# Hybrid encoder trunk: both heads of a pair walked together in the attention mixers, the state space scan given out in four phases

## The chip, the cores and the metric

One Trainium2 chip, one core. Its engines run side by side: TensorE (PE, with its weight loads as PEld), VectorE (DVE), ScalarE (ACT), GpSimd (POOL) and SyncE (SP), which issues the loads from HBM. Each has its own queue and works through it in order; between engines semaphores set the order. The metric is the device time of one execution in microseconds (us).

## The reference

Two layers over 512 tokens of width 1024, in float32. The mixers of a layer are what the change touches:

```python
for i in range(DEPTH):
    h = rms_norm(x, g_mix[i])
    x = x + hybrid_mixer(h, ...)
    h = rms_norm(x, g_ffn[i])
    x = x + (swiglu(h, ...) if i % 2 == 0 else moe_swiglu(h, ...))
    x = x + (p[i] @ ple_w_up[i]) * sigmoid(rms_norm(x, g_ple[i]) @ ple_w_gate[i])

def hybrid_mixer(h, ...):
    (u, fq, fk, fv, ff, cq, ckv, kpe, dq, dk, dv) = split(h @ w_in)
    y_a = s5_mixer(u, ...)                              # state space scan, then GLU
    y_b = fox_mixer(fq, fk, fv, ff, b_f)                # 4 heads, decay, frame causal
    y_c = mla_mixer(cq, ckv, kpe, ...)                  # 4 heads, low rank, chunk causal
    y_d = chunk_band_attention(dq, dk, dv, rel_bias)    # 4 heads, relative bias
    for bi, y in enumerate((y_a, y_b, y_c, y_d)):
        merged += sigmoid(h @ w_gate[bi] + b_gate[bi]) * (y @ w_branch[bi])
    return merged @ w_o
```

The attention mixers: for each head, softmax(q k^T / sqrt(d) + bias or decay, masked) times v. The scan: x_t = a x_(t-1) + B u_t over complex states, y = C x + D u, then y = gelu(y), y * sigmoid(y @ w_glu).

## The kernel before

All activations lie transposed in SBUF (features on partitions, 512 tokens along the row). Dense projections get float32 accuracy from two parts of each operand: `mm3` (lines 153 to 155) issues three matmuls, hi*hi, hi*lo, lo*hi. A weight tile is loaded by SP (`load`, line 130), its hi part is cast by ACT (line 133), its lo part by DVE (line 135); a ring holds four such tiles. PSUM has two pools of four banks: pool a (`bank_a`), from which the projections take theirs, and pool b (`bank_b`), from which scores, transposes, value products and the scan take theirs. A pool gives its banks out in turn, in the order of the program's text.

A scheduler orders the instructions of each engine when the program is built. It may put later instructions, such as projections that need only a bank of pool a and a weight tile, between the steps of an earlier part that has to wait.

A layer's mixer runs in the text in this order: the values of chk (branch 3); two chk pairs (`unit_chk`), with `s5_prep` after the first (it builds the tables of the scan in `s5_maps`, DVE lines 355 to 392); the gates and products of branch 3; two fox pairs (`unit_fox`), the gates and products of branch 1; two mla pairs (`unit_mla`); the scan (`s5`); gates and products of branch 2; gates and products of branch 0. `gates` runs eight projections, 24 matmuls each; `product` eight of six matmuls.

`attention` handles one head; a pair calls it twice. It goes through four query blocks b of 128 rows, with n = 128(b+1) keys. For each: scores on PE (line 580), a mask on PE for fox (582) and mla (584) or a bias added by DVE for chk (589), the maximum on DVE (591), the exponential with its sum on ACT (592), the reciprocal (593) and the scaling (594) on DVE, one transpose on PE for each 128 keys (597) into a bank of pool b, the evacuation to PT by ACT or DVE in turn by block (600, 602), and the value products on PE (604), which put the head's 64 rows on its half of yps. So there are 96 such blocks in the program: two layers, three kinds of attention, four heads, four blocks.

`s5` stands in one piece: u (466), the maps W on PE (472), the vector work and the scan on DVE (484 to 499), y4 on PE (506 to 508), gelu, the copies to gT (514), the GLU's matmuls on PE (518). The matmul of an attention or the scan has float32 operands; the trace has two records for many of these.

Of the kernel before, what the change touches and what calls it, by code (L numbers as in the profile page):

```python
# [11 lines left out]
F = mybir.dt.float32  # L12
# [3 lines left out]
AF = mybir.ActivationFunctionType  # L16
OP = mybir.AluOpType
AX = mybir.AxisListType
# [4 lines left out]
S = 512  # L23
# [20 lines left out]
def trunk(ctx, tc, I, out, dbg=None):  # L44
    nc = tc.nc
    act = nc.scalar.activation
    tt = nc.vector.tensor_tensor
    ts = nc.vector.tensor_scalar
# [3 lines left out]
    mm = nc.tensor.matmul  # L52
# [13 lines left out]
    small = pool("small", 2)  # L66
# [4 lines left out]
    def bank_a():  # L71
        return pa.tile([128, 512], F, name="a", tag="a")

    def bank_b():
        return pb.tile([128, 512], F, name="b", tag="b")
# [23 lines left out]
    ident = cst[:, 0:128]  # L99
# [140 lines left out]
    ident_b = const.tile([128, 128], BF, name="ident_b")  # L240
    caus_b = const.tile([128, 128], BF, name="caus_b")
    tri_b = const.tile([128, 128], BF, name="tri_b")
    onesm_b = const.tile([128, 128], BF, name="onesm_b")
    half_b = const.tile([1, 128], BF, name="half_b")
    neg_b = const.tile([1, 64], BF, name="neg_b")
# [202 lines left out]
    def s5(l, u_src, yT, tt_pool):  # L448
        with new_pool("s5") as p:
            def tile8(nm, tag=None):  # L450
                return p.tile([128, 8, 128], F, name=nm, tag=tag or nm)
# [12 lines left out]
            for g in range(4):  # L464
                for j in range(4):
                    cp[(4 * g + j) % 3](U4[32 * j:32 * j + 32, g::4, :], u5[32 * g:32 * g + 32, :, :, j])
            wps = []
            for c, PT in enumerate((PT0, PT1)):
                for h in range(2):
                    ps = bank_b()  # L470
                    for a in range(4):
                        mm(ps[:, a * 128:(a + 1) * 128], PT[:, 4 * h + a, :], U4[:, 4 * h + a, :],
                           start=True, stop=True)
# [17 lines left out]
            for z, w in ((zr, W[0]), (zi, W[1])):  # L491
                nc.vector.tensor_tensor_scan(out=fl(w), data0=fl(R), data1=fl(z), initial=0.0,
                                             op0=OP.mult, op1=OP.add)
            Xr, Xi = zr, zi
            for Xc, a, b, o in ((Xr, 0, 1, OP.subtract), (Xi, 1, 0, OP.add)):
                nc.vector.memset(Xc[:, :, 0:1], 0.0)
                tt(out=Xc[:, :, 1:128], in0=Er[:, :, 0:127], in1=W[a][:, :, 0:127], op=OP.mult)
                tt(out=z1[:, :, 0:127], in0=Ei[:, :, 0:127], in1=W[b][:, :, 0:127], op=OP.mult)
                tt(out=Xc[:, :, 1:128], in0=Xc[:, :, 1:128], in1=z1[:, :, 0:127], op=o)
            y4 = tile8("y4", "z1")  # L500
            for h in range(2):
                ps = bank_b()
# [9 lines left out]
            for g in range(4):  # L512
                for i in range(4):
                    cp[(4 * g + i) % 3](g5[32 * g:32 * g + 32, :, :, i], y4[32 * i:32 * i + 32, g::4, :])
            for m in range(2):
                ps = bank_b()
                for k in range(2):
                    mm(ps, wg[:, k, m * 128:(m + 1) * 128], gT[:, k, :], start=(k == 0), stop=(k == 1))
                th_ = p.tile([128, S], F, name="th", tag=f"W{m}")
                act(th_, ps, AF.Tanh, scale=0.5)  # L520
                stt(th_, th_, 1.0, gT[:, m, :], op0=OP.add, op1=OP.mult)
                split(th_, yT[0][:, m, :], yT[1][:, m, :], scale=0.5)
# [48 lines left out]
            tt(out=xs, in0=xs, in1=ps, op=OP.add)  # L571
        return f

    def attention(ap, kind, qk, V, vh, yps, a, T):
        for b in range(4):
            n = 128 * (b + 1)
            s = bank_b()
            qs = slice(b * 128, (b + 1) * 128)
            for i, (qT, kT) in enumerate(qk):
                mm(s[:, :n], qT[:, qs], kT[:, :n], start=(i == 0), stop=(kind == "chk" and i == len(qk) - 1))  # L580
            if kind == "fox":
                mm(s[:, n - 128:n], ident_b, caus_b, start=False, stop=True)
            if kind == "mla":
                mm(s[:, n - 64:n], half_b, neg_b, start=False, stop=True)
            mx = small.tile([128, 2], F, name="mx", tag="mx", bufs=6)
            src = s
            P = ap.tile([128, S], F, name="P", tag="P", bufs=3)
            if kind == "chk":
                tt(out=P[:, :n], in0=s[:, :n], in1=T[:, S - n:S], op=OP.add)
                src = P  # L590
            nc.vector.tensor_reduce(out=mx[:, 0:1], in_=src[:, :n], axis=AX.X, op=OP.max, negate=True)  # L591
            act(P[:, :n], src[:, :n], AF.Exp, bias=mx[:, 0:1], accum_out=mx[:, 1:2])  # L592
            nc.vector.reciprocal(mx[:, 1:2], mx[:, 1:2])
            ts(P[:, :n], P[:, :n], mx[:, 1:2], None, op0=OP.mult)
            pt = bank_b()
            for kb in range(b + 1):
                nc.tensor.transpose(pt[:, kb * 128:(kb + 1) * 128], P[:, kb * 128:(kb + 1) * 128], ident)
            PT = ap.tile([128, S], F, name="PT", tag="PT", bufs=3)
            if b % 2:
                act(PT[:, :n], pt[:, :n], AF.Copy)  # L600
            else:
                nc.vector.tensor_copy(PT[:, :n], pt[:, :n])
            for kb in range(b + 1):
                mm(yps[64 * a:64 * a + 64, qs], V[:, kb, vh * 64:(vh + 1) * 64], PT[:, kb * 128:(kb + 1) * 128],  # L604
                   start=(kb == 0), stop=(kb == b))

    def mixer(l, N, nxt):
        with ExitStack() as mx_stack:
# [19 lines left out]
            def y_tiles():  # L628
                return (yp.tile([128, 2, S], FR, name="y_hi", bufs=2), yp.tile([128, 2, S], FR, name="y_lo", bufs=2))

            def gates(bi, dst, after=None):
                g = []
                for m in range(NK):
                    ps = bank_a()
                    w = load(I["w_gate"][l, bi, m], [128, NK, 128], after=after if m < 3 else None)
                    for k in range(NK):
                        mm3(ps, at(w, ALL, k, ALL), at(hT, ALL, k, ALL), start=(k == 0), stop=(k == NK - 1))
                    t_ = dst(m)
                    act(t_, ps, AF.Tanh, scale=0.5, bias=bg[:, bi, m:m + 1])
                    g.append(t_)  # L640
                return g
# [24 lines left out]
            ap = at_stack.enter_context(new_pool("at"))  # L666
# [83 lines left out]
            def unit_chk(cp, pr, V, yT):  # L750
                q2 = [qk_tile(cp, f"dq{a}", 9) for a in range(2)]

                def cq(ps):
                    for a in range(2):
                        own, oth = halves(a)
                        act(q2[a][own], ps[own], AF.Copy, scale=0.125)
                    for a in range(2):
                        own, oth = halves(a)
                        stt(q2[a][oth], ps[own], 0.125, q2[a][own].bitcast(F), op0=OP.mult, op1=OP.subtract)

                in_tile(l, 6 + pr, hT, cq, hi_after=evacs[3] if pr else None)
                k2 = [qk_tile(cp, f"dk{a}", 9) for a in range(2)]
                kl = qk_tile(cp, "dl", 9)

                def ck(ps):
                    for a in range(2):
                        own, oth = halves(a)
                        act(k2[a][own], ps[own], AF.Copy)
                        act(k2[a][oth], ps[own], AF.Copy)
                    for a in range(2):  # L770
                        own = halves(a)[0]
                        marks.append(tt(out=kl[own], in0=ps[own], in1=k2[a][own].bitcast(F), op=OP.subtract))

                in_tile(l, 8 + pr, hT, ck, hi_after=evacs[3] if pr else None)
                yps = bank_b()
                for a in range(2):
                    h = 2 * pr + a
                    own = halves(a)[0]
                    T = cp.tile([128, S], F, name="T", tag="T", bufs=2)
                    nc.sync.dma_start(out=T, in_=I["chk_T"][l, h])  # L780
                    nc.vector.memset(T[0:64, 448:512], NEG)
                    attention(ap, "chk", [(q2[a], k2[a]), (q2[a][own], kl[own])], V, h, yps, a, T)
                split(yps, yT[0][:, pr, :], yT[1][:, pr, :])

            def unit_fox(fp, pr, V, yT):
# [22 lines left out]
                in_tile(l, 4 + pr, hT, con(1.0, cumk, 1))  # L808
                yps = bank_b()
                (q1, q2), (k1, k2) = tiles  # L810
                for a in range(2):
                    attention(ap, "fox", [(q1[a][0:96], k1[a][0:96]), (q2[a], k2[a])], V, 2 * pr + a, yps, a, None)
                split(yps, yT[0][:, pr, :], yT[1][:, pr, :])

            def unit_mla(mp, pr, V, yT, wuq, wuk):
# [22 lines left out]
                    nc.vector.tensor_copy(ks[a][0:64], ps[64 * a:64 * a + 64])  # L838
                    nc.gpsimd.tensor_copy(ks[a][64:96], krot[32 * a:32 * a + 32])
                yps = bank_b()  # L840
                for a in range(2):
                    attention(ap, "mla", [(qs[a][0:96], ks[a][0:96])], V, 2 * pr + a, yps, a, None)
                split(yps, yT[0][:, pr, :], yT[1][:, pr, :])

            V = values(1)
# [43 lines left out]
                in_tile(l, m, hT, lambda ps: act(dst, ps, AF.Copy))  # L889

            yA = y_tiles()
            s5(l, u_src, yA, tp)
            g = gates(2, ring)
            product(2, yC, g, False)
            g = gates(0, ring)
            product(0, yA, g, False)
            tp_stack.close()
            mT = hT
# [989 lines left out]
```

## Time and profile before

| | us |
|---|---|
| median of three runs | 2049.72 |
| lowest, highest of the three | 2049.27, 4567.53 |
| profiled execution, its own time | 2048.55 |
| span of the profiled execution | 2046.8 |

The mean granted clock of PE in the profiled execution is 0.995 of full speed. In layer 0 the chk stage lies at 56 to 189 us of the span, fox at 189 to 262, mla at 262 to 358, the scan and its neighbours behind it up to about 425; layer 1 repeats them some 929 us later. The stretch 650 to 700 lies in layer 0's feed-forward part and holds projections alone. Times in the rows are us from the start of the span; "busy" counts an instruction from its start to its modelled end, so that the busy times of consecutive matmuls overlap, and a price for one is read from start to start.

### The profile page before, as it was taken

Reading aid. Unit: us, or ns where it says so; the run is one execution under the profiler, and the core shown is the slowest. Engines: PE = TensorE matmul, PEld = TensorE weight load, DVE = VectorE, ACT = ScalarE, POOL = GpSimd, SP = SyncE. Lnnn points to the kernel's source line nnn. Section 1 sums busy time; section 2 is a strip of 40 time slices with the busy share of each in tenths; the row PEclk is TensorE's granted clock in tenths of the full one; section 3 lists DMA queues with packets and bytes.
Section 4 is the critical chain, followed back from the end, with each engine's and each line's share of the span. In section 5 each row is a group of like instructions: output and inputs, shape, how many; then the busy total and the mean of one; then the engine's idle time right before and its main releaser. Section 6 shows DMA issues by size and latency. Waiting matters only on the chain. (4 is left out here: it accounts for less than half of the span.)

```text
span 2046.8 us, 27188 instructions
## 1 busy us (share of the span) xinstructions
PE 1988.4 (97%) x9922; PEld 1545.7 (76%) x9922; DVE 1195.5 (58%) x1849; ACT 910.4 (44%) x1345; POOL 317.7 (16%) x616
## 2 busy tenths in 40 slices
PE   7999999899999999999999999999999999999998
PEld 7787777688888888888777776778677777667566
DVE  6766454836332333335666554736799986656574
ACT  6434433333322222244434433333578875556454
POOL 2058020302000000001048120202100000000011
PEclk9999999999999999999999999999999999999899
DMA  5332121333533333422332121335589996758542
GB/s 178 100 102 90 62 88 56 119 108 103 185 93 89 107 93 93 124 86 62 120 116 83 63 88 52 121 111 204 205 340 363 370 364 254 260 207 315 199 166 105
DMA packets 94563, 309.23 MB, mean 151 GB/s; under 512 B 12161, under 2 KB 15105, under 8 KB 94402
## 3 DMA queue, kind: packets, MB, share of 16 engines
q1 hardware_dynamic: 89218, 289.40, 40.9%
q0 software_dynamic: 5040, 17.44, 2.5%
q8 instruction: 99, 1.62, 0.3%
q14 instruction: 62, 0.51, 0.1%
q10 hardware_dynamic: 144, 0.26, 0.0%
HBM read 283.46 MB, written 23.60 MB: 150 GB/s over the span
## 5 line engine op out<-in xcount | busy, mean ns | idle before, releaser
L133 ACT ACTIVATE whi<-wraw 128x1024 fp32r<-128x1024 f32 (+2 forms) x211 | 217.3, 1033 | 479.1 <-PE a L154 302.8
L135 DVE TENSOR_TENSOR wlo<-wraw,whi 128x1024 fp32r<-128x1024 f32 (+2 forms) x211 | 258.5, 1232 | 282.3 <-ACT whi L133 276.5
L153 PE MATMUL a<-hT_hi,whi 128*128 128x512 f32 (+3 forms) x1056 | 415.8, 395 | 0.7 <-ACT hT_hi L159 0.7
L155 PE MATMUL a<-hT_hi,wlo 128*128 128x512 f32 (+3 forms) x1056 | 415.6, 394 | 0.0
L154 PE MATMUL a<-hT_lo,whi 128*128 128x512 f32 (+3 forms) x1056 | 414.3, 393 | 0.7 <-DVE hT_lo L159 0.6
L1289 DVE TENSOR_TENSOR wlo<-raw,whi 128x1024 fp32r<-128x1024 f32 (+1 forms) x198 | 228.1, 1160 | 50.1 <-ACT whi L1287 42.7
L153 PEld LDWEIGHTS a<-hT_hi,whi 128*128 128x128 f32 (+1 forms) x1056 | 196.8, 187 | 46.2 <-issue 4.8
L155 PEld LDWEIGHTS a<-hT_hi,wlo 128*128 128x128 f32 (+1 forms) x1056 | 197.0, 187 | 45.2 <-issue 4.5
L154 PEld LDWEIGHTS a<-hT_lo,whi 128*128 128x128 f32 (+1 forms) x1056 | 197.0, 187 | 45.0 <-issue 3.5
L1287 ACT ACTIVATE whi<-raw 128x1024 fp32r<-128x1024 f32 (+1 forms) x198 | 199.1, 1010 | 54.9 <-PE a L1336 32.3
L655 POOL TENSOR_TENSOR A<-A,t 128x512 f32<-128x512 f32 x48 | 80.3, 1703 | 278.5 <-DVE t L654 278.5
L153 PE MATMUL a<-whi,hT_hi 128*128 128x256 f32 (+2 forms) x328 | 110.7, 337 | 1.0 <-ACT hT_hi L159 1.0
L155 PE MATMUL a<-whi,hT_lo 128*128 128x256 f32 (+2 forms) x328 | 109.0, 333 | 0.3
L154 PE MATMUL a<-wlo,hT_hi 128*128 128x256 f32 (+2 forms) x328 | 108.8, 332 | 0.0
L1336 PE MATMUL a<-whi,heA_hi 128*128 128x512 f32 (+1 forms) x304 | 93.7, 389 | 6.1 <-PEq L1696 3.3
L1336 PE MATMUL a<-whi,heA_lo 128*128 128x512 f32 (+1 forms) x304 | 90.8, 380 | 0.9 <-issue 0.9
L1336 PE MATMUL a<-wlo,heA_hi 128*128 128x512 f32 (+1 forms) x304 | 90.8, 380 | 0.0
L604 PE MATMUL b<-PT,V 128*64 128x128 f32 x480 | 73.0, 283 | 2.8 <-ACT PT L600 2.7
L604 PEld LDWEIGHTS b<-PT,V 128*64 128x64 f32 x480 | 49.8, 136 | 33.7 <-ACT PT L600 15.6
L592 ACT ACTIVATE P<-b,mx 128x128 f32<-128x128 f32 (+1 forms) x64 | 33.8, 527 | 91.3 <-DVE mx L591 91.0
L1336 PEld LDWEIGHTS a<-whi,heA_hi 128*128 128x128 f32 x304 | 54.9, 191 | 24.4 <-issue 9.9
L153 PEld LDWEIGHTS a<-whi,hT_hi 128*128 128x128 f32 x328 | 62.3, 190 | 7.7 <-ACT hT_hi L159 1.5
(525 smaller groups left out, 3562.8 us busy)
## 6 DMA issues: line engine op xcount, KB each, us to landing
raw<-in_moe_w13a SPq DMA_DIRECT2D x113, 512.0 KB, 7.3
raw<-in_moe_w SPq DMA_DIRECT2D x74, 512.0 KB, 8.2
wraw<-in_w_gate SPq DMA_DIRECT2D x64, 512.0 KB, 3.6
wraw<-in_ffn_w SPq DMA_DIRECT2D x64, 512.0 KB, 3.6
raw<-in_moe_w13b SPq DMA_DIRECT2D x61, 384.0 KB, 6.2
wraw<-in_w_in_T SPq DMA_DIRECT2D x20, 512.0 KB, 3.8
wraw<-in_w_branch SPq DMA_DIRECT2D x16, 512.0 KB, 3.6
wraw<-in_w_o SPq DMA_DIRECT2D x16, 512.0 KB, 3.6
```

What stands on the lines that cost most here:

```text
L133: act(hi[:, :n], raw[:, :n], AF.Copy)
L135: tt(out=lo[:, :n], in0=raw[:, :n], in1=hi[:, :n].bitcast(F), op=OP.subtract)
L153: mm(o, a[0], b[0], start=start, stop=False)
L154: mm(o, a[0], b[1], start=False, stop=False)
L155: mm(o, a[1], b[0], start=False, stop=stop)
L592: act(P[:, :n], src[:, :n], AF.Exp, bias=mx[:, 0:1], accum_out=mx[:, 1:2])
L604: mm(yps[64 * a:64 * a + 64, qs], V[:, kb, vh * 64:(vh + 1) * 64], PT[:, kb * 128:(kb + 1) * 128], start=(kb == 0), stop=(kb == b))
L655: gtt(out=A[m], in0=A[m], in1=g[m], op=OP.add)
L1287: act(hi[:, :w], raw[:, :w], AF.Copy)
L1289: return tt(out=lo[:, :w], in0=raw[:, :w], in1=hi[:, :w].bitcast(F), op=OP.subtract)
L1336: mm(dst[x][:, :w_], st[sa][:, k, :], w[:, cs[x]], start=first and q == 0, stop=last and q == 2)
```

## The change

`attention` now takes both heads of a pair. In each block it issues scores and softmax of the first head (a = 0), then of the second, then the transposes of the first into a bank of pool b, evacuated by DVE, then those of the second into a bank of pool a, evacuated by ACT. The transposed probabilities go back into P, so PT is gone, and P has six buffers in place of three. The value products alternate between the heads, which write the two halves of yps. In chk both bias tiles are loaded ahead of the pair. `s5` is a generator with three yields; its four phases are given out before the gates of branch 2, at the second of them, and at the second and sixth of the gates of branch 0.

```diff
+            yield                      # s5, after the copies to U4
             wps = []
...
+            yield                      # after the scan
             y4 = tile8("y4", "z1")
...
+            yield                      # after the copies to gT
             for m in range(2):
                 ps = bank_b()
...
-    def attention(ap, kind, qk, V, vh, yps, a, T):
+    def attention(ap, kind, qks, V, vhs, yps, Ts=None):
         for b in range(4):
             n = 128 * (b + 1)
-            s = bank_b()
             qs = slice(b * 128, (b + 1) * 128)
...
+            PTs = []
+            for a, qk in enumerate(qks):
+                s = bank_b()
...
+                P = ap.tile([128, S], F, name="P", tag="P", bufs=6)
...
+                PTs.append(P)
+            for a in range(2):
+                P = PTs[a]
+                pt = (bank_b, bank_a)[a]()
+                for kb in range(b + 1):
+                    nc.tensor.transpose(pt[:, kb * 128:(kb + 1) * 128], P[:, kb * 128:(kb + 1) * 128], ident)
+                if a:
+                    act(P[:, :n], pt[:, :n], AF.Copy)
+                else:
+                    nc.vector.tensor_copy(P[:, :n], pt[:, :n])
             for kb in range(b + 1):
-                nc.tensor.transpose(pt[:, kb * 128:(kb + 1) * 128], P[:, kb * 128:(kb + 1) * 128], ident)
-            PT = ap.tile([128, S], F, name="PT", tag="PT", bufs=3)
-            if b % 2:
-                act(PT[:, :n], pt[:, :n], AF.Copy)
-            else:
-                nc.vector.tensor_copy(PT[:, :n], pt[:, :n])
-            for kb in range(b + 1):
-                mm(yps[64 * a:64 * a + 64, qs], V[:, kb, vh * 64:(vh + 1) * 64], PT[:, kb * 128:(kb + 1) * 128],
-                   start=(kb == 0), stop=(kb == b))
+                for a in (1, 0):
+                    vh = vhs[a]
+                    mm(yps[64 * a:64 * a + 64, qs], V[:, kb, vh * 64:(vh + 1) * 64], PTs[a][:, kb * 128:(kb + 1) * 128],
+                       start=(kb == 0), stop=(kb == b))
...
-            def gates(bi, dst, after=None):
+            def gates(bi, dst, after=None, between={}):
                 g = []
                 for m in range(NK):
+                    if m in between:
+                        next(between[m], None)
                     ps = bank_a()
...
-            s5(l, u_src, yA, tp)
-            g = gates(2, ring)
+            scan = s5(l, u_src, yA, tp)
+            next(scan)
+            g = gates(2, ring, between={1: scan})
             product(2, yC, g, False)
-            g = gates(0, ring)
+            g = gates(0, ring, between={1: scan, 5: scan})
             product(0, yA, g, False)
```

In the new text the scores are line 585, the masks 587 and 589, the maximum 596, the scaling 599, the transposes 605, the evacuations 607 and 609, the value products 613, y4's matmuls 508 to 510.

How the instructions stand on PE in the last block of a fox pair of layer 0, before: L597 are transposes, L580 scores, L582 the mask, L604 value products, L153 to L155 projections.

```order
L155 MATMUL a<-hT_hi,wlo 128x512
L153 MATMUL a<-hT_hi,whi 128x512
L597 MATMUL b<-cst,P 128x128 x3
L580 MATMUL b<-f1c_2042,f0c_1999 128x512
L580 MATMUL b<-f1s_2044,f0s_2001 128x512
L582 LDWEIGHTS ident_b
L582 MATMUL b<-caus_b,ident_b 128x128
L154 MATMUL a<-hT_lo,whi 128x512
L604 MATMUL b<-PT,V 64x128 x3
L155 MATMUL a<-hT_hi,wlo 128x512
L153 MATMUL a<-hT_hi,whi 128x512
```

The same place on PE now: L605 are the transposes (into pool b for the first head, pool a for the second), L585 the scores, L587 the mask, L613 the value products.

```order
L605 MATMUL b<-cst,P 128x128 x3
L585 MATMUL b<-f1c_2026,f0c_1983 128x512
L605 MATMUL a<-cst,P 128x128 x3
L585 MATMUL b<-f1s_2028,f0s_1985 128x512
L587 LDWEIGHTS ident_b
L587 MATMUL b<-caus_b,ident_b 128x128
L585 MATMUL b<-f1c_2027,f0c_1984 128x512
L585 MATMUL b<-f1s_2029,f0s_1986 128x512
L613 MATMUL b<-P,V 64x128 x6
L587 LDWEIGHTS ident_b
L587 MATMUL b<-caus_b,ident_b 128x128
L605 MATMUL b<-cst,P 128x128 x4
```

The projections of lines 153 to 155 that stood between the steps are gone from this place; the first ones stand behind the second head's last transposes (three ahead of the pair's last value products, the rest behind them).

DVE in the first chk pair of layer 0, between the third and the fourth block, before: L355 to L360 belong to s5_maps, L772 to the keys of the second pair, L135 is a weight cast, L589 the bias, L591 the maximum, L593 and L594 reciprocal and scaling, L602 the evacuation.

```order
L602 COPY PT<-b 128x384
L589 TENSOR_TENSOR P<-b,T 128x512
L355 TENSOR_TENSOR gd_966<-PB,bz 128x128
L591 TENSOR_REDUCE mx<-P 128x1
L356 TENSOR_TENSOR gd_967<-PB,bz 128x128
L772 TENSOR_TENSOR dl<-a,dk_1316 64x512
L772 TENSOR_TENSOR dl<-a,dk_1317 64x512
L593 RECIPROCAL mx<-mx 128x1
L135 TENSOR_TENSOR wlo<-wraw,whi 128x1024
L594 TENSOR_SCALAR P<-P,mx 128x512
```

The same place on DVE now: L594 is the bias, L596 the maximum, L598 and L599 reciprocal and scaling, L609 the evacuation.

```order
L609 COPY P<-b 128x384
L594 TENSOR_TENSOR P<-b,T 128x512
L360 TENSOR_TENSOR Pi<-gd_894,gd_895 128x4x32
L596 TENSOR_REDUCE mx<-P 128x1
L594 TENSOR_TENSOR P<-b,T 128x512
L355 TENSOR_TENSOR gd_902<-PB,Pr 128x128
L596 TENSOR_REDUCE mx<-P 128x1
L598 RECIPROCAL mx<-mx 128x1
L356 TENSOR_TENSOR gd_903<-PB,Pi 128x128
L599 TENSOR_SCALAR P<-P,mx 128x512
```

Two heads' blocks stand where one stood, with operations of s5_maps still between their steps. Between the first maximum of the first pair and that of the second, DVE has the same operations of s5_maps as before (L355 to L360 eight times each, and the rest) and four weight casts in place of ten.

PE at the start of y4 in layer 0, before: L507 is one of y4's three matmuls, the others are projections of the product of branch 2.

```order
L154 MATMUL a<-y_lo,whi 128x512
L155 MATMUL a<-y_hi,wlo 128x512
L507 MATMUL b<-zr,sd_3204 128x128 x2
L153 MATMUL a<-y_hi,whi 128x512
L154 MATMUL a<-y_lo,whi 128x512
```

And now, where L508 to L510 are y4's matmuls:

```order
L154 MATMUL a<-hT_lo,whi 128x512
L155 MATMUL a<-hT_hi,wlo 128x512
L508 MATMUL b<-U_3170,sd_3158 128x128
L509 MATMUL b<-zr,sd_3156 128x128
L510 MATMUL b<-zi,sd_3157 128x128
L508 MATMUL b<-U_3170,sd_3158 128x128
```

Between the maps and y4 there are now 240 projection matmuls, and between y4 and the GLU's first matmul 96, where eight stood.

## Rows read from the trace of the kernel before

**Rows 1.** The page, part 1: busy time, share of span, instructions of each engine

```profile
PE 1988.4 (97%) x9922; PEld 1545.7 (76%) x9922; DVE 1195.5 (58%) x1849; ACT 910.4 (44%) x1345; POOL 317.7 (16%) x616
```

**Rows 2.** Windows: length, busy PE, PEld, DVE, ACT, POOL; PE clock, DMA share, GB/s

```profile
56.00:189.00 133.00, 130.32 (x658) 101.08 (x657) 92.93 (x234) 53.24 (x97) 59.16 (x165) 1.00 0.31 100
189.00:262.00 73.00, 71.09 (x362) 52.34 (x361) 37.59 (x76) 33.36 (x66) 16.71 (x46) 1.00 0.21 65
262.00:358.00 96.00, 96.00 (x451) 68.69 (x449) 48.71 (x93) 30.84 (x62) 14.39 (x12) 1.00 0.22 70
650.00:700.00 50.00, 50.00 (x222) 41.22 (x221) 14.38 (x16) 9.83 (x11) 0.00 (x0) 1.00 0.31 95
...
59.00:128.00 69.00, 68.64 (x334) 52.33 (x333) 50.99 (x138) 25.86 (x45) 5.59 (x16) 1.00 0.33 102
```

**Rows 3.** Timeline of all engines, one mla block: start, length, instruction, idle before

```profile
326.96 0.70 PE L580 MATMUL b<-mk,mq 96*128 96x256 f32 x2
...
327.83 0.43 DVE L591 TENSOR_REDUCE mx<-b 128x1 f32<-128x256 f32 x1 [1.53 <-PE b L584]
...
328.35 0.47 ACT L592 ACTIVATE P<-b,mx 128x256 f32<-128x256 f32 x1 [3.60 <-DVE mx L591]
...
329.15 0.35 DVE L594 TENSOR_SCALAR P<-P,mx 128x256 f32<-128x256 f32 x1
...
329.67 0.39 PE L597 MATMUL b<-cst,P 128*128 128x128 f32 x2
...
329.89 0.81 PE L580 MATMUL b<-mk,mq 96*128 96x384 f32 x2
```

**Rows 4.** Groups by form, PE, of chk, fox, mla in turn: busy, mean ns

```profile
L155 PE MATMUL a<-hT_hi,wlo 128*128 128x512 f32 x103 | 41.3, 401 | 0.0
...
L155 PE MATMUL a<-whi,hT_lo 128*128 128x256 f32 x32 | 9.5, 298 | 0.0
...
L154 PE MATMUL a<-y_lo,whi 128*128 128x512 f32 x16 | 6.4, 401 | 0.6 <-DVE y_lo L159 0.6
...
L153 PE MATMUL a<-hT_hi,whi 128*128 128x512 f32 x65 | 26.7, 411 | 0.0
...
L155 PE MATMUL a<-hT_hi,wlo 128*128 128x512 f32 x66 | 26.9, 408 | 0.0
```

**Rows 5.** Timeline of PE: value products of one mla block, then a projection

```profile
341.04 1.09 PE L604 MATMUL b<-PT,V 128*64 128x128 f32 x8
342.06 0.50 PE L153 MATMUL a<-hT_hi,whi 128*128 128x512 f32 x1
```

**Rows 6.** Groups by form: whole span, then weight casts at 59 to 128 us

```profile
L591 DVE TENSOR_REDUCE mx<-b 128x1 f32<-128x512 f32 x16 | 11.1, 691 | 7.4 <-PE b L584 7.4
...
L592 ACT ACTIVATE P<-b,mx 128x512 f32<-128x512 f32 x16 | 11.0, 687 | 31.7 <-DVE mx L591 31.7
...
L135 DVE TENSOR_TENSOR wlo<-wraw,whi 128x1024 fp32r<-128x1024 f32 x10 | 12.2, 1220 | 5.3 <-ACT whi L133 3.6 <-ACT P L592 1.6
```

**Rows 7.** Timeline of PE in the experts: matmuls of 64 columns, alternate halves

```profile
1755.59 2.37 PE L1340 MATMUL b<-raw,yh 128*64 128x512 f32 x10
```

**Rows 8.** Timeline of PE in the scan: y4 and GLU of layer 0, GLU of layer 1

```profile
389.49 0.71 PE L507 MATMUL b<-zr,sd 128*128 128x128 f32 x4 [1.11 <-DVE zr L499]
...
405.61 6.63 PE L518 MATMUL b<-gT,wglu 128*128 128x512 f32 x8 [3.71 <-DVE gT L514]
...
1335.03 2.38 PE L518 MATMUL b<-gT,wglu 128*128 128x512 f32 x5 [3.73 <-DVE gT L514]
```

**Rows 9.** Windows around stops of PE (as rows 2), and one timeline row

```profile
404.80:411.50 6.70, 5.89 (x7) 2.52 (x8) 5.34 (x7) 1.23 (x2) 2.17 (x1) 0.50 0.37 102
1325.00:1335.00 10.00, 6.29 (x40) 5.24 (x39) 9.83 (x15) 6.54 (x9) 5.90 (x4) 1.00 0.33 105
1896.50:1906.50 10.00, 7.89 (x18) 6.08 (x19) 3.46 (x3) 3.06 (x3) 1.27 (x3) 0.50 0.51 194
...
1903.21 1.01 PE L1336 MATMUL a<-whi,heA_lo 128*128 128x512 f32 x2 [0.94 <-issue]
```

More of the change, by code (lines that the diff above doesn't have):

```diff
@@ L572, in residual @@
         return f
-    def attention(ap, kind, qk, V, vh, yps, a, T):
+    def attention(ap, kind, qks, V, vhs, yps, Ts=None):
         for b in range(4):
             n = 128 * (b + 1)
-            s = bank_b()
             qs = slice(b * 128, (b + 1) * 128)
[L579 to L595, printed above, removed]
-            for kb in range(b + 1):
-                nc.tensor.transpose(pt[:, kb * 128:(kb + 1) * 128], P[:, kb * 128:(kb + 1) * 128], ident)
-            PT = ap.tile([128, S], F, name="PT", tag="PT", bufs=3)
-            if b % 2:
-                act(PT[:, :n], pt[:, :n], AF.Copy)
-            else:
-                nc.vector.tensor_copy(PT[:, :n], pt[:, :n])
-            for kb in range(b + 1):
-                mm(yps[64 * a:64 * a + 64, qs], V[:, kb, vh * 64:(vh + 1) * 64], PT[:, kb * 128:(kb + 1) * 128],
-                   start=(kb == 0), stop=(kb == b))
@@ new lines, in attention @@
+            PTs = []
+            for a, qk in enumerate(qks):
+                s = bank_b()
+                for i, (qT, kT) in enumerate(qk):
+                    mm(s[:, :n], qT[:, qs], kT[:, :n], start=(i == 0), stop=(kind == "chk" and i == len(qk) - 1))
+                if kind == "fox":
+                    mm(s[:, n - 128:n], ident_b, caus_b, start=False, stop=True)
+                if kind == "mla":
+                    mm(s[:, n - 64:n], half_b, neg_b, start=False, stop=True)
+                mx = small.tile([128, 2], F, name="mx", tag="mx", bufs=6)
+                src = s
+                P = ap.tile([128, S], F, name="P", tag="P", bufs=6)
+                if kind == "chk":
+                    tt(out=P[:, :n], in0=s[:, :n], in1=Ts[a][:, S - n:S], op=OP.add)
+                    src = P
+                nc.vector.tensor_reduce(out=mx[:, 0:1], in_=src[:, :n], axis=AX.X, op=OP.max, negate=True)
+                act(P[:, :n], src[:, :n], AF.Exp, bias=mx[:, 0:1], accum_out=mx[:, 1:2])
+                nc.vector.reciprocal(mx[:, 1:2], mx[:, 1:2])
+                ts(P[:, :n], P[:, :n], mx[:, 1:2], None, op0=OP.mult)
+                PTs.append(P)
@@ L775, in unit_chk @@
                 yps = bank_b()
+                Ts, qks = [], []
                 for a in range(2):
-                    h = 2 * pr + a
                     own = halves(a)[0]
                     T = cp.tile([128, S], F, name="T", tag="T", bufs=2)
-                    nc.sync.dma_start(out=T, in_=I["chk_T"][l, h])
+                    nc.sync.dma_start(out=T, in_=I["chk_T"][l, 2 * pr + a])
                     nc.vector.memset(T[0:64, 448:512], NEG)
-                    attention(ap, "chk", [(q2[a], k2[a]), (q2[a][own], kl[own])], V, h, yps, a, T)
+                    Ts.append(T)
+                    qks.append([(q2[a], k2[a]), (q2[a][own], kl[own])])
+                attention(ap, "chk", qks, V, (2 * pr, 2 * pr + 1), yps, Ts)
                 split(yps, yT[0][:, pr, :], yT[1][:, pr, :])
@@ L810, in unit_fox @@
                 (q1, q2), (k1, k2) = tiles
-                for a in range(2):
-                    attention(ap, "fox", [(q1[a][0:96], k1[a][0:96]), (q2[a], k2[a])], V, 2 * pr + a, yps, a, None)
+                attention(ap, "fox", [[(q1[a][0:96], k1[a][0:96]), (q2[a], k2[a])] for a in range(2)], V,
+                          (2 * pr, 2 * pr + 1), yps)
                 split(yps, yT[0][:, pr, :], yT[1][:, pr, :])
@@ L840, in unit_mla @@
                 yps = bank_b()
-                for a in range(2):
-                    attention(ap, "mla", [(qs[a][0:96], ks[a][0:96])], V, 2 * pr + a, yps, a, None)
+                attention(ap, "mla", [[(qs[a][0:96], ks[a][0:96])] for a in range(2)], V, (2 * pr, 2 * pr + 1), yps)
                 split(yps, yT[0][:, pr, :], yT[1][:, pr, :])
```

## The prediction

> **What bounds the kernel now.** I read the busy shares first, then the attention stages of layer 0 window by window, then single blocks on the timeline. TensorE (PE) is busy 97% of the span and no other engine over 58% [rows 1], so a change pays only if PE's total gets shorter or if PE waits less, and it costs as soon as PE waits where it does not now. In the windows of layer 0's three attention stages (chk, fox, mla) PE is busy for 130.32 of 133, 71.09 of 73 and 96.00 of 96 us, at full clock [rows 2]. Yet the softmax of one block takes long: in an mla block of 256 keys the scores begin at 326.96, the maximum at 327.83, the exponential at 328.35, the scaling at 329.15, the transposes at 329.67, the next scores at 329.89 [rows 3]. That is 2.93 us from scores to next scores, of which PE works about 1 on this head: the scores 0.64, mask and transposes the rest. PE does not stand still because the scheduler has put projection matmuls of later gates and values in between. So the first thing to ask of the new order is whether that filler is still there.
>
> **The filler.** The order rows answer this. In the old fox pair, one to seven projection matmuls stand between any two steps; in the new one the pair runs from its first score to the last transposes with none, and only three or four stand before the last products. The reason is the bank of the second head: its transposes now take a bank of pool a, from which the projections take theirs, so these queue behind them in turn. The projections do not vanish; they come after the pair, in runs of 68 to 285. PE then gets through the same projections in the same time, but the waits of the softmax chain lie open in all twelve pairs (two layers, three stages, two pairs).
>
> **What attention costs PE now.** A projection matmul of 512 columns takes 50.00 / 222 = 0.225 us [rows 2], one of 256 columns half, 0.113 as an estimate. chk: 103 x 3 and 16 x 3 wide ones are 357, 80.3 us; 96 narrow ones 10.8; s5_maps' 48 matmuls of 128 columns, at the 0.128 of rows 5, 6.1; of 133 us 35.8 remain, 17.9 a pair [rows 2, 4]. fox: 65 x 3 = 195, 43.9; 29.1 remain, 14.6 a pair. mla: 66 + 65 + 66 and the 48 of the product are 245, 55.1; 54 further ones, about half of them wide, 9.1; 31.8 remain, 15.9 a pair.
>
> **What a pair costs without filler.** The chain for n = 256 is 2.93; per 128 columns more the maximum grows by 0.13 (0.43 to 0.69 for 256 more), the exponential by 0.11 [rows 3, 6], scaling, scores and transposes by about 0.1 each, an estimate: some 0.52. So the four blocks take 2.40 + 2.93 + 3.45 + 3.97 = 12.75. Both heads' softmax run side by side, one chain ahead of the other; to it come the other head's transposes and mask that stand between (0.55), the first products, which wait for an evacuation ahead of the next scores (1.15), the tail (last evacuation 0.6 and four pairs of products 1.0), and the entry, in which q and k are evacuated before the first score, since nothing else is there to do (two 512-column operations at 0.69 and the hops between engines: 2.1). That is 18.1; fox's shorter scores bring it to 17.5; I take 17.8 for both. The eight fox and mla pairs: 8 x 17.8 - 4 x (14.6 + 15.9) = **+20 us**. The bounds: entry and tail covered by what little filler is left, 8 x 14.1, -9; or DVE's casts of the next weights (1.22 us each [rows 6]) falling into every pair once, +30.
>
> **chk is longer.** There s5_maps' vector work stands in DVE's order between the attention steps (second order excerpt) and in PE's way. DVE is busy 50.99 us between the two pairs' first scores [rows 2], 12.2 of it in ten casts [rows 6]. The new order has the same map and attention operations there and four casts: 50.99 - 6 x 1.22 = 43.7, and about 4 of waits: 48 us. The second pair takes 18, the entry 2.8: 69, less the narrow projections and the maps that PE still does in it (16.9): 52 against 35.8. Twice: **+33 us**. Lower bound: if the maps stay out of the chain, two pairs of 17.8, nothing; upper: ten casts as before, +47.
>
> **The paired products.** Eight product instructions take 1.02 us [rows 5], 0.128 each; there are 480 records of them (two for each of 240), 61 us in all. If the two column halves run at once, half of it, 31 us, is off PE. The trace has such a pair already: matmuls of 64 columns on alternate halves, 512 wide, ten in 2.37 us, 0.24 each [rows 7], where alone they would take 4 x 0.128 = 0.51. So I believe in the halving, 2.6 a pair; but PE is no longer what a pair waits for, and it shows in the tail alone, where it is counted. The moved evacuations (DVE always the first head, ACT the second), the six buffers of P in place of three and three, and the bias tiles loaded ahead lie beside the chain: nothing; uncovered, one bias load would be a few us per chk pair.
>
> **The scan in phases.** Its stops now: 1.11 us before the second half of y4, 3.71 and 3.73 before the GLU [rows 8], and about 1.2 in small ones, 6 a layer. In the new order 240 projection matmuls (54 us) stand before y4 and 96 (21.6 us) before the GLU, where eight stood; the vector work that they hide, the chain now ending in the 3.71 us stop, is far shorter than that. All of it goes, and with it the half clock behind layer 0's stop, 6.7 us [rows 9], 3.4 back: 2 x 6 + 3.4 = 15.4, **-16 us**. SP and POOL are not in it; the loads keep their order but for s5's few. Bounds: -10 if y4's stop stays, -18.
>
> Sum with the clock held: 33 + 20 - 16 = +37, on 2048.55 of the profiled execution (its span 2046.8; the runs' median, 2049.72, is 1.2 over it): **2086**.
>
> **The clock.** It fell to 0.50, 1.2 GHz in place of 2.4, after the 3.71 us stop before layer 0's GLU and once in a stage of the experts, and stayed there for 6.70 and 10.0 us, though PE was busy for 5.89 and 7.89 of them; it stayed at 1.00 in layer 1, where PE was busy 6.29 of 10 us, a 3.73 us stop at their end [rows 8, 9]. A pair's entry and first two blocks hold about 1.5 and 2.5 us of PE work, both heads' together, in 2.1 + 2.4 + 2.9 us: 0.54, sparser than that, but in shorter pieces than a stop of 3.7. So I expect a fall in three pairs of four, of the length that the two rows show: 8.35 us on average, of which half is lost, 4.2. Nine falls, and one less for chk's first pairs, which DVE bounds: 8 x 4.2 = +34, **2120**. Bounds: none, 0; low through the whole pair: PE's own 12.0 to 15.3 us (the above less 2.6) doubled are 25 in fox and mla, 7.5 over the 17.8, and 30.6 in chk's second pair, 12.6 over: 8 x 7.5 + 2 x 12.6 = +85.
> The Trainium skill (TensorE: Matmul & The Clock Gate, "Loop structure matters more than you think") says that the loop nest decides whether matmuls stay warm, and that a wait between matmuls makes them run cold; its example waits for a DMA, this nest for a softmax. By that rule every pair would be cold, 2171; by the row of layer 1 none, 2086.
>
> **The rivals.**
> - The clock holds: PE's share in a pair, 12 to 13 of 17.8, is above the 0.63 at which it held. 2086. Against it: the share is uneven, and lowest at the start.
> - The clock is low through each pair: 2171. For it: the second low stretch went on through a stop of 0.94 us [rows 9]. Against: a pair's last blocks are dense.
> - The halves don't run at once, so the change does not do what it says: 0.51 in place of 0.26 for each of the four pairs of products in the tail, 12 x 1.0 = +12 on the forecast, 2132. Rows 7 speak against it.
> - The other side: PE isn't kept waiting. If other work covers the chain, in spite of the order, pairing gives its 31 and the phases 16: 2049 - 47 = 2002. It decides where the walk of a pair is shorter than PE's work in it, 12.0 to 13.3 us; with 12.75 for the bare chain that needs entry and tail to be hidden altogether.
>
> **How the numbers follow.** Forecast .46 (its own range 2098 to 2145), clock held .28, clock low .16, halves apart .05, other side .05. About 2% can be told from no change here: 2007.6 and 2089.5 are the limits. Slower: .46 + .16 + .05 less a few hundredths of the forecast, and a third of the clock-held case, whose terms spread by 20 us: .73. Faster .05, same .22. The range runs from 2060, the clock-held case with most of chk's term gone, to 2174, just above the clock-low case; it leaves out the other side, the lowest of the clock-held and the highest rest.
>
> **What would show it.** PE's idle time in layer 0's attention windows, 4.6 us now [rows 2], should grow to over 40, most of it before the transposes and released by DVE's scaling; the granted clock should be under 1 in some of the fox and mla pairs; the GLU's stop should be gone; the 480 products should show half the start-to-start time. If PE's idle time hardly grows, the filler argument is wrong. If it grows as said and the clock is 1.00 throughout, the clock step is. If chk's windows lengthen no more than fox's, the maps were no bound.

## The result, and the profile after

The changed kernel takes 2185.93 us (2185.11 to 2188.94, four runs) against 2049.49; the ratio is 1.067, with a 95% interval of 1.065 to 1.069. It is slower by 136 us, as forecast in sign, and lies 12 us above the top of the range that was given, 66 above the forecast. One of the four runs before, of 4567.53 us, is left out of the ratio.

The page of the changed kernel, parts 1 and 2: busy times, and PE's granted clock in 40 slices, in tenths.

```profile
PE 2031.1 (93%) x9922; PEld 1582.5 (72%) x9922; DVE 1189.0 (54%) x1849; ACT 908.9 (42%) x1345; POOL 306.6 (14%) x616
...
PEclk9769796899999999999769887799999999999999
```

The span grew from 2046.8 to 2184.0 us, by 137.2. PE's busy time grew by 42.7 [rows 1], although the paired products shorten it, and its idle time (span less busy) from 58.4 to 152.9, by 94.5. The clock dips in two places, the attention stages of the two layers. Its mean over the span is 0.932; with 1.00 and 0.50 as the only levels that is 0.068 x 2184 / 0.5 = 297 us at 1.2 GHz.

PE's waits, costliest first: what waits, for what, us in total, times, longest.

```profile
PE b L605 <- DVE P L599: 45.9, 39, 3.7
PE b L605 <- DVE mx L598: 17.6, 9, 3.7
PE b L189 <- DVE xn L178: 12.6, 7, 7.8
PE b L585 <- DVE dl L783: 8.7, 7, 3.9
PE b L585 <- DVE mq L847: 8.4, 4, 2.1
PE b L585 <- ACT f1c L811: 7.9, 6, 1.5
PE b L585 <- ACT dk L780: 6.1, 4, 2.1
```

The third row (the norms) is as before. Before, the transposes waited for the scaling too, but seldom:

```profile
PE b L597 <- DVE P L594: 3.8, 6, 0.9
```

The waits for the reciprocal and of the first scores for q and k are new, but for 0.3 us. The two stops before the GLU [rows 8] are gone.

Windows of the six pairs of layer 0 from the first score to the last products, chk, fox, mla in turn (columns as in [rows 2]).

```profile
61.00:91.90 30.90, 20.43 (x87) 13.46 (x88) 22.35 (x71) 9.21 (x24) 0.27 (x1) 0.56 0.22 64
111.80:144.90 33.10, 20.61 (x82) 12.95 (x80) 21.04 (x56) 8.34 (x23) 31.04 (x94) 0.50 0.11 40
223.60:244.90 21.30, 14.89 (x89) 10.28 (x90) 12.78 (x33) 8.30 (x25) 0.00 (x0) 0.76 0.09 25
256.60:278.40 21.80, 15.72 (x89) 11.02 (x90) 12.35 (x32) 8.26 (x24) 0.00 (x0) 0.69 0.08 25
339.50:368.30 28.80, 23.32 (x89) 12.97 (x89) 11.44 (x31) 6.77 (x21) 1.22 (x2) 0.53 0.00 1
373.00:402.00 29.00, 23.08 (x89) 12.70 (x90) 11.42 (x31) 6.70 (x20) 0.00 (x0) 0.53 0.14 52
```

The clock falls in every one of them. With 1.00 and 0.50 as the only levels it is low for 27 to 33 us of a chk pair, 10 to 14 of a fox pair and 27 of an mla pair. In mla that is nearly the whole pair, though PE is busy 80% of it, and a pair takes 29 us where 15.7 (17.8 less the entry) were forecast at full clock. Inside such a pair, the timeline of all engines for the block that answers to [rows 3]:

```profile
378.45 1.22 PE L585 MATMUL b<-mk,mq 96*128 96x256 f32 x2
...
379.61 0.23 PE L589 MATMUL b<-neg_b,half_b 1*128 1x64 bf16 x1
...
379.88 0.42 DVE L596 TENSOR_REDUCE mx<-b 128x1 f32<-128x256 f32 x1 [2.58 <-PE b L589]
380.39 0.47 ACT L597 ACTIVATE P<-b,mx 128x256 f32<-128x256 f32 x1 [2.62 <-DVE mx L596]
...
381.19 0.43 DVE L596 TENSOR_REDUCE mx<-b 128x1 f32<-128x256 f32 x1 [0.89 <-PE b L589]
381.53 0.15 DVE L598 RECIPROCAL mx<-mx 128x1 f32<-128x1 f32 x1
...
381.72 0.36 DVE L599 TENSOR_SCALAR P<-P,mx 128x256 f32<-128x256 f32 x1
...
382.13 0.69 PE L605 MATMUL b<-cst,P 128*128 128x128 f32 x2 [0.98 <-DVE P L599]
```

Each of DVE's and ACT's steps takes what it took. From scores to transposes it is 3.68 us in place of 2.71, and two stretches make the difference. From the scores' start to the mask PE takes 1.16 us (378.45 to 379.61) in place of 0.64. And from the exponential to the scaling it is 1.33 us in place of 0.80: on DVE the second head's maximum (381.19) stands ahead of the first head's reciprocal, and it waits 0.89 us for the second head's scores on PE. In e1 below, with the same order on DVE at full clock, such a block has 0.79 (297.44 to 298.23). PE is not only late because it waits; it is slow in what the softmax then waits for.

### The profile page after: what moved, and what is told of

The parts are those of the page before. It is cut to its first block, busy times and chain, and to the rows that moved or that the text cites. A ratio compares the mean times of both kernels' runs of the same rounds, so it can differ in the third digit from the quotient of the medians.

```text
span 2184.0 us, 27189 instructions
## 1 busy us (share of the span) xinstructions
PE 2031.1 (93%) x9922; PEld 1582.5 (72%) x9922; DVE 1189.0 (54%) x1849; ACT 908.9 (42%) x1345; POOL 306.6 (14%) x616
## 5 line engine op out<-in xcount | busy, mean ns | idle before, releaser
L135 DVE TENSOR_TENSOR wlo<-wraw,whi 128x1024 fp32r<-128x1024 f32 (+2 forms) x211 | 255.6, 1215 | 438.6 <-ACT whi L133 427.5
L153 PE MATMUL a<-hT_hi,whi 128*128 128x512 f32 (+3 forms) x1056 | 412.7, 392 | 0.8 <-ACT hT_hi L159 0.8
L155 PE MATMUL a<-hT_hi,wlo 128*128 128x512 f32 (+3 forms) x1056 | 409.4, 388 | 0.0
L153 PEld LDWEIGHTS a<-hT_hi,whi 128*128 128x128 f32 (+1 forms) x1056 | 197.7, 188 | 43.5 <-ACT hT_hi L159 1.5
L155 PEld LDWEIGHTS a<-hT_hi,wlo 128*128 128x128 f32 (+1 forms) x1056 | 197.5, 187 | 42.3
L666 POOL TENSOR_TENSOR A<-A,t 128x512 f32<-128x512 f32 x48 | 72.9, 1554 | 447.7 <-DVE t L665 447.7
L153 PE MATMUL a<-whi,hT_hi 128*128 128x256 f32 (+2 forms) x328 | 110.4, 337 | 1.0 <-ACT hT_hi L159 1.0
L155 PE MATMUL a<-whi,hT_lo 128*128 128x256 f32 (+2 forms) x328 | 108.9, 333 | 0.3
L605 PE MATMUL b<-cst,P 128*128 128x128 f32 x120 | 35.2, 413 | 63.5 <-DVE P L599 45.9
L605 PEld LDWEIGHTS b<-cst,P 128*128 128x128 f32 x120 | 19.0, 199 | 73.5 <-issue 46.2
L596 DVE TENSOR_REDUCE mx<-b 128x1 f32<-128x128 f32 (+3 forms) x64 | 31.5, 492 | 68.9 <-PE b L589 47.1
L597 ACT ACTIVATE P<-b,mx 128x128 f32<-128x128 f32 (+3 forms) x64 | 33.8, 528 | 82.7 <-DVE mx L596 82.1
```

The lines of the kernel that those rows point to most:

```text
L135: tt(out=lo[:, :n], in0=raw[:, :n], in1=hi[:, :n].bitcast(F), op=OP.subtract)
L153: mm(o, a[0], b[0], start=start, stop=False)
L155: mm(o, a[1], b[0], start=False, stop=stop)
L666: gtt(out=A[m], in0=A[m], in1=g[m], op=OP.add)
```

## Experiments

**The bank.** One line of the changed kernel:

```diff
-                pt = (bank_b, bank_a)[a]()
+                pt = bank_b()
```

> One edit to the changed kernel (2185.9 us): the transposes of the second head take a bank of pool b, as those of the first do. In the order the projection matmuls are back between the steps of a pair: 28 to 85 a pair, where the changed kernel has 3 or 4 and the kernel before 65 to 158. If the loss comes from the filler that the pool a bank drove out of the pairs, nearly all of it goes: no waits in the fox and mla pairs, granted clock 1.00 there, and then the halved value products (31 us) and the phases of the scan (16) remain as gains: 2000 to 2015 us, under the 2049.5 of before. Rival: the loss comes from walking two heads together as such (two softmax chains on one DVE, six buffers of P): then the time stays over 2120 us.

1986.64 us, 0.970 of the kernel before (0.9685 to 0.9717), and 199 us below the changed kernel. Windows of e1 over the two fox pairs and the two mla pairs of layer 0, and its first waits of PE:

```profile
178.40:221.00 42.60, 42.18 (x265) 29.92 (x265) 30.97 (x73) 24.75 (x60) 15.30 (x39) 1.00 0.20 63
271.60:313.20 41.60, 41.60 (x242) 27.73 (x242) 27.76 (x66) 15.86 (x44) 1.21 (x2) 1.00 0.21 77
```

```profile
PE b L189 <- DVE xn L178: 12.3, 7, 7.9
PE a L1349 <- PEq L1709: 3.4, 1, 3.4
PE a L153 <- ACT hT_hi L159: 1.7, 5, 0.7
```

No wait of the softmax is left, and the clock is 1.00. Walking two heads together, six buffers of P and the in-place evacuation are all still there, so the loss doesn't come from them; the one line of the bank takes it away. Two more kernels take the bank of pool a once a pair, in the last block or in the first:

```diff
-                pt = (bank_b, bank_a)[a]()
+                pt = bank_a() if a and b == 3 else bank_b()     # e6; b == 0 in e7
```

> The kernel of e1 with the second head's transposes in a bank of pool a in the last block alone (one bank of pool a a pair in place of four). If the bank works through its turn, the projections of later gates, whose banks come behind it, can't be ahead of that block: the order has 0 to 4 of them in a pair, as in the changed kernel, and the time is the changed kernel's, 2170 to 2195 us. If the loss came from the number of pool a banks taken, or from their evacuation by the second engine, three quarters of it go: about 2035 us.

2207.53 us, 12 above what was expected. One bank at the end of a pair costs all that four cost, and 22 us more. Most of that lies in the fox pairs, which take 26 us in place of 21.5, at a clock of 0.61 in place of 0.69 to 0.76; why it is low for longer there is open. The first of them:

```profile
223.60:250.10 26.50, 18.95 (x89) 12.54 (x89) 12.68 (x33) 8.21 (x23) 0.00 (x0) 0.61 0.06 20
```

> The kernel of e1 with the second head's transposes in a bank of pool a in the first block alone. By the turn, the projections are kept out only up to that block and come in behind it: 9 to 44 a pair in the order, about half of e1's or more. The entry and the first chain lie open, some 4 us in each of twelve pairs, and the clock falls in a few of them: 2020 to 2070 us. By the number of banks, as e6.

2103.12 us: between e1 and e6, as the turn says and the number of banks doesn't, but 33 us above what was expected. Two windows of e7 show where, the first mla pair of layer 0 and the second from its second block on (its first block's scores still stand inside the first pair):

```profile
315.30:343.90 28.60, 22.95 (x104) 12.77 (x104) 16.61 (x42) 8.79 (x27) 1.22 (x2) 0.76 0.00 1
345.20:362.30 17.10, 17.10 (x103) 11.30 (x102) 9.41 (x22) 6.59 (x17) 0.00 (x0) 1.00 0.01 2
```

The first pair, with 13 projection matmuls within it, has a low clock for half of it and takes 28.6 us; the stretch of the second, with 28, has a full one and takes 17.1.

**The clock.** Three kernels keep the changed order and fill PE's waits with matmuls that change no result (`filler` holds the activations hT): six per block ahead of the first head's transposes (e4), the same in the first two blocks alone (e8), and five per block with ten at a pair's entry (e9).

```diff
+        for _ in range(10):                                     # e9 alone, into yps
+            mm(yps, filler[0][:, 0, 0:128], filler[0][:, 0, :], start=True, stop=True)
         for b in range(4):
...
                 pt = (bank_b, bank_a)[a]()
+                for _ in range(5 if a == 0 else 0):             # e4: 6; e8: 6 and b < 2
+                    mm(pt, filler[0][:, 0, 0:128], filler[0][:, 0, :], start=True, stop=True)
```

> The changed kernel with six further matmuls of 128x512 per block, ahead of the first head's transposes, into the bank that these overwrite: 288 x 2 = 576... in all 48 blocks x 6 = 288 matmuls, 65 us of PE time at full clock, which change no result and stand where PE waits for the softmax; the projections between the steps stay as few as in the changed kernel (3 or 4 a pair). If the half clock sets most of the loss, the clock holds at 1.00 in most pairs, a fox pair takes 16 to 18 us in place of 21.5 and an mla pair 17 to 19 in place of 28.8: 2100 to 2130 us in spite of more work. If the open waits alone set it and the clock does not matter, the added matmuls cost nothing or up to 65 us: 2186 to 2250 us.

2166.92 us: 19 less than the changed kernel with 288 more matmuls, but 37 above what was expected. The mean clock is 0.966, so 147 us are still low; it did not hold.

> The changed kernel (2185.9 us) with the six added matmuls of e4 in the first two blocks of each pair alone, 144 matmuls and 32 us of PE time at full clock. If the clock falls because the entry and the first two blocks are sparse, as the prediction argued, and holds once it is kept up there, it is low for less time than in e4 (147 us) and the time is under e4's 2166.9 less the saved work: 2120 to 2145 us. If a pair's later blocks drop it as well, it is low for about as long as in the changed kernel (300 us) and the time is 2175 to 2215.

2169.98 us, between the two expectations, with a mean clock of 0.950, 217 us low, in the profiled one of its two runs and 0.957 in the other. Filling the first blocks alone holds the clock less than filling all does; in time the two kernels can't be told apart, since e8's runs lie at 2163.84 and 2176.12.

> The changed kernel (2185.9 us) with added matmuls of 128x512 that change no result: ten at the entry of each pair, where PE waits for q and k, and five per block ahead of the first head's transposes, 30 a pair, 360 in all, 81 us of PE time at full clock. The projections between the steps stay 3 or 4 a pair. Theory: entry and gaps both filled, the clock holds at 1.00 through the fox and mla pairs, and each takes 16 to 20 us from its first score to its last products, with more PE work in it than the changed kernel's 21.5 and 28.8: 2110 to 2150 us, the clock low for under 100 us. Rival: the softmax chain alone needs the 21 and 29 us: the pairs are no shorter, and the time is 2186 or more.

2111.22 us: 75 us less than the changed kernel with 360 more matmuls, 81 us of PE's time at 0.225. The mean clock is 0.987, 55 us low. The six pairs of layer 0:

```profile
60.20:80.00 19.80, 17.45 (x101) 11.20 (x101) 16.70 (x58) 9.12 (x23) 0.86 (x4) 1.00 0.13 34
110.10:129.20 19.10, 17.33 (x102) 11.00 (x102) 15.21 (x47) 8.35 (x24) 17.45 (x52) 1.00 0.16 59
208.20:225.60 17.40, 16.34 (x111) 11.51 (x111) 11.86 (x33) 7.64 (x23) 0.00 (x0) 1.00 0.10 31
237.60:255.20 17.60, 16.24 (x111) 11.45 (x110) 11.62 (x32) 7.76 (x23) 0.00 (x0) 1.00 0.11 31
316.50:336.20 19.70, 18.82 (x113) 12.71 (x113) 11.21 (x30) 6.75 (x21) 1.22 (x2) 1.00 0.00 1
341.00:363.60 22.60, 21.35 (x109) 13.64 (x110) 11.19 (x30) 6.78 (x21) 0.00 (x0) 0.85 0.18 68
```

Five hold 1.00, and every one is shorter than in the changed kernel: chk 19.8 and 19.1 in place of 30.9 and 33.1, fox 17.4 and 17.6 in place of 21.3 and 21.8, mla 19.7 and 22.6 in place of 28.8 and 29.0. In sum 116.2 in place of 164.9 us, 49 in this layer, with some 20 of the 30 added matmuls, 4.5 us, inside each. So at least 75 of the 136 us come from the low clock, since the added work, apart from holding the clock, can only have cost time. The sixth pair is the exception that shows the start: only six of its ten entry matmuls stand right ahead of it, and its entry stayed half open.

```profile
341.09 0.46 PE L589 MATMUL b<-mk,mq 96*128 96x128 f32 x2 [0.74 <-DVE mq L854]
341.48 0.20 PE L593 MATMUL b<-neg_b,half_b 1*128 1x64 bf16 x1
342.53 0.46 PE L589 MATMUL b<-mk,mq 96*128 96x128 f32 x2 [0.85 <-DVE mk L858]
```

No single stop is over 0.9 us there, and the clock fell. The same pair of layer 1 has the same two stops, 0.74 and 0.85 us, and falls as well. Its window, and the longest low stretch of e9 in layer 0, between the chk pairs:

```profile
1302.00:1325.90 23.90, 22.71 (x109) 14.52 (x109) 11.13 (x30) 6.70 (x20) 0.00 (x0) 0.79 0.16 63
...
95.10:108.70 13.60, 6.65 (x28) 6.39 (x29) 9.70 (x31) 1.01 (x2) 1.89 (x5) 0.50 0.27 78
```

**The maps in chk.** `s5_prep` moved behind the second chk pair, its first DVE operations tied to that pair's end (`unit_chk` returns it now):

```diff
                 for pr in range(2):
-                    unit_chk(cp, pr, V, yD)
-                    if pr == 0:
-                        if l == 0:
-                            setup_ssm()
-                        s5_prep(l, marks[1])
+                    done = unit_chk(cp, pr, V, yD)
+                if l == 0:
+                    setup_ssm()
+                s5_prep(l, done[1])
```

> The changed kernel with s5_prep moved behind the second chk pair, so that none of s5_maps' vector operations stands in DVE's order between attention steps; they lie under the projections that follow. By the prediction's chk step DVE bounds the stretch between the two pairs' first scores (48 us forecast, 50.8 measured) and the maps are some 25 us of that: the stretch shrinks to 25 to 35 us, and of that the part that the projections and maps on PE do not need, 8 to 12 us a layer, comes off the time: 2162 to 2170 us. Rival: PE's half clock sets the chk pairs too, and the maps were hidden in it: 2180 to 2190.

2177.84 us, 8 less, between the two expectations. The stretch between the two pairs' first scores is 43.2 us in place of 50.8:

```profile
59.40:102.60 43.20, 30.76 (x124) 21.34 (x124) 21.68 (x50) 14.06 (x31) 1.02 (x4) 0.64 0.16 49
```

DVE is busy for half of it, so it is no bound any more, but the pair still walks at half clock and takes 30.6 of the 43.2. With the clock held and the maps in place, in e9, the stretch is 49.9 (60.2 to 110.1), though the walk in it is 19.8, and PE's wait ahead of the maps' matmuls is 18.0 us in all, in two places, where the changed kernel has 3.0 (through it DVE works on the maps and the second pair's q and k):

```profile
PE b L374 <- issue: 18.0, 2, 9.2
```

So the maps and the clock each bound this stretch; taking one away leaves the other.

**The scan, and the products' pairing.**

> The kernel before with the scan's four phases and nothing of the attention. By the sum's own term the scan's stops before y4 and before the GLU go, with the half clock after one: 16 us, 2033 us, and the waits before the GLU (7.4 us in two stops) are gone from the trace. Rival: another wait takes their place, or the GLU's matmuls were no loss: 2049 us, no change.

2037.88 us, ratio 0.9946 (0.993 to 0.9963): a gain of 10.2 us in place of 16, small but clear of the spread of the runs. The GLU's waits and those before y4 are gone; two of the waits that stand instead:

```profile
PE a L153 <- DVE t L659: 2.5, 2, 1.3
PE a L1342 <- ACT whi L1293: 2.5, 1, 2.5
```

The first stands where y4 begins, in both layers; whether the second, in the experts, has to do with the edit was not tried.

> The changed kernel with the scan in one piece again, as before. If the two parts add up, the scan's 16 us come back on top of 2185.9: 2202 us, with the attention pairs as in the changed kernel (fox 21 to 22 us, mla 29, half clock). If the phases are a part of the loss, it is faster than 2186.

2196.81 us, 10.9 above the changed kernel: the phases are worth the same with either attention, and no part of the loss.

> The kernel of e1 (1986.6 us) with one edit: the value products of the second head all stand ahead of those of the first, as before, in place of alternating. The projections between the steps are the same in number (28 to 85 a pair). Where PE is the bound, as in e1 (its waits in the pairs are gone), two halves that run at once are worth half of the products' time, 31 us by the sum's term: 2018 us, and the products' start-to-start time doubles again. If the halves do not run at once, or something else sets e1's gain: 1987 us.

```diff
-            for kb in range(b + 1):
-                for a in (1, 0):
+            for a in (1, 0):
+                for kb in range(b + 1):
```

1997.71 us: alternation is worth 11 us in e1, a third of what was expected. The last products of the second mla pair of layer 0 on the timeline of PE, e1 first, then e5, and the projection behind them:

```profile
311.99 1.09 PE L613 MATMUL b<-P,V 128*64 128x128 f32 x16
313.01 0.50 PE L153 MATMUL a<-hT_hi,whi 128*128 128x512 f32 x1
```

```profile
316.87 1.58 PE L613 MATMUL b<-P,V 128*64 128x128 f32 x16
318.38 0.50 PE L153 MATMUL a<-hT_hi,whi 128*128 128x512 f32 x1
```

Sixteen records take 1.02 us from start to start with alternation, as eight did before [rows 5]: the halves do run at once. Without it they take 1.51, not 2.04: the first head's matmuls begin beside the second head's last ones once the two groups stand next to each other. Summed over all 480 records, from each start to the next start on PE, the products take 68 us before, 45 in e5 and 35 in e1. So 23 of the 33 us gained on them come from bringing the two heads together, and 10 from alternating.

> The changed kernel with the second head's value products ahead of the first's in place of alternating (the edit of e5, there worth 11 us). If in the changed kernel PE waits for the softmax and only each pair's tail is open, alternation is worth the tail alone, 1 to 2 us at half clock in each of twelve pairs at most, or less: 2186 to 2205. If PE at half clock is the bound within the mla pairs, where it is busy 81%, its worth is twice e5's there: about 2200 as well; if alternation is worth nothing: 2186.

2194.19 us, 8 above: within what was expected, and too near both readings to tell them apart.

## Why the prediction was right or wrong

- **The filler: right.** The order had 3 or 4 projections in a pair, the softmax's waits appeared, and PE's idle time in the six pairs of layer 0 is 47 us (164.9 less the 118.0 busy), where a sign was set at over 40. e1, e6 and e7 tie all this to the turn of pool a's banks.
- **The clock: the step that failed.** It took a fall in three pairs of four, 8.35 us long, +34 us. The clock fell in all twelve pairs, for some 287 of the 297 low us: 10 to 14 us in a fox pair, not far from that length, but 27 and more in each chk and mla pair. Against the 2111.2 of e9 the low clock costs at least 75 us, since e9 also does 81 us of added work; half of 287, 143 us, is the most that it can have cost. The two rows that gave 8.35 us [rows 9] were low stretches that ended in dense work. The 0.94 us stop in one of them already stood in the text as evidence for the clock-low case: that case, at 2171 with a chance of .16, is the one that happened, 15 us short. That it comes so near is partly luck: it gave every fox and mla pair 25 us, and from the first score alone fox takes 21.3 and 21.8, mla 28.8 and 29.0; the first chk pairs, which it left out, fell too. The Trainium skill (TensorE: Matmul & The Clock Gate, "Loop structure matters more than you think") says that the loop nest decides whether matmuls stay warm. The windows agree: every pair has a clock under 0.8, and here no DMA is in the waits, where the section's example has one of 8 us.
- **Fox and mla's walk: nearly right at full clock.** 15.7 us without the entry were forecast; e9 has 17.4, 17.6 and 19.7 with about 4.5 us of added matmuls inside. At the clock that was granted it is 21.3 to 29.0. The term, +20, was priced at a speed that PE did not have.
- **chk: half right.** The stretch to the second pair's first score was forecast at 48 and is 50.8, and in e9 49.9, so with the clock held DVE's maps do bound it. The second pair was forecast at 18 and takes 33.1, 19.1 with the clock held: the clock again.
- **The products: right, in size too.** At once they run, and the 31 us forecast off PE are 33 in e1; 10 of them are alternation's own. The time says the same: alternation is worth 11 us in e1, where PE is the bound, and 8 in the changed kernel, where the forecast counted the tail alone.
- **The scan: right in sign, -16 for a measured -10.** The stops went; the small ones that the sum counted as gone stayed, and two new ones of 2.5 us in all came.
- **The other side (2002): not this kernel, but e1.** It is what the walk gives when the filler is there, and it came out at 1986.6, below that rival's own price. Of its 61 us over the kernel before, 10 are the phases and about 33 the products. The rest was not taken apart.

## What to carry to other kernels

A scheduler fills one engine's waits only with work whose buffers are granted in time: before giving a step a bank of another pool, ask whose turn comes behind it. Where matmuls stand sparsely for tens of microseconds, reckon with the low clock for most of them (here nearly a whole chk or mla pair, and half of a fox pair), not with the length of earlier falls that dense work cut short. A wait that is opened on TensorE costs twice: the wait itself, and the slower matmuls that the waiting chain needs.

## What the runs showed of the hardware

- The clock fell to 0.50 in pairs without any stop near the 3.7 us of before [rows 8]: in the changed kernel the longest stop of PE in a fox pair is 1.5 us and in an mla pair 2.1, and in e9's second mla pairs the clock fell after stops of 0.74 and 0.85 us, in both layers. It stayed low with PE busy 80% of an mla pair.
- Added matmuls made a kernel faster: 360 of them, 81 us of work, took 75 us off.
- Products of two heads on two column halves overlap in part even without alternation: 1.51 us for sixteen records, against 1.02 alternating and 1.02 for eight alone.
